# Second block's experts: PSUM banks emptied one to three chunks later in the issue order, six tiles of split halves and eight chunk buffers

## The chip, the core and the metric

The kernel runs on one core of one Trainium2 chip. The metric is the device time of the whole kernel in microseconds (us), the median of several runs. TensorE (PE) multiplies, with its weight loads shown apart (PEld); VectorE (DVE) and ScalarE (ACT) split weights and empty PSUM banks; SyncE (SP) issues the loads from HBM, in order.

## The reference, cut to what matters

Two transformer blocks in sequence on x of shape (1, 256, 1024), float32. The second block has two layers; the second of these ends in a mixture of experts, the stage at issue:

```python
D_MODEL, N_EXPERTS_2, D_FF_EXPERT, TOP_K = 1024, 8, 3584, 2

def swiglu(x, w_gate, w_up, w_down):
    return (jax.nn.silu(x @ w_gate) * (x @ w_up)) @ w_down

def moe_swiglu(x, router, w_gate, w_up, w_down):
    logits = (x @ router).astype(jnp.float32)
    top_val, top_idx = lax.top_k(logits, TOP_K)
    top_w = jax.nn.softmax(top_val, axis=-1)
    combine = jnp.sum(jax.nn.one_hot(top_idx, N_EXPERTS_2, dtype=jnp.float32) * top_w[..., None], axis=-2)
    out = jnp.zeros_like(x)
    for e in range(N_EXPERTS_2):
        out = out + combine[..., e:e + 1].astype(x.dtype) * swiglu(x, w_gate[e], w_up[e], w_down[e])
    return out
```

Each expert has 3 x 1024 x 3584 float32 weights, 44 MB, so the eight are 352 MB to be read from HBM.

## The kernel before

The kernel runs its stages one after the other; the experts of the second block are `moe2`. The router's result is ranked, and the experts are taken in the order of their token counts. The six with most tokens are **wide** (up to 128 tokens each, index p = 0 to 5), the last two are **narrow**: they share one tile of 128 rows, 64 for each.

Weights come in **chunks** of 128 x 2048 float32 (1 MB), loaded by SP into a ring of buffers `raw` (`load`, L309). For a wide expert `weights` (L346) takes a chunk and `split` (L332) makes of each half a high part `wh` (a cast on ScalarE, L340) and a low part `wl` (a subtraction on VectorE, L341), in a ring of tiles `hl`. `mm3` (L367 to L371) multiplies three times: low by high, high by low, high by high. One chunk is 12 matmuls of 512 columns. With four pairs in `hl` two chunks can be split at a time; the phase gives ten chunk buffers (six of its own, four shared), and two spare tiles (`once`) are used once each at the start.

The outer loop runs over n = 0 to 41, seven slices f of the hidden width for each of six wide experts. `up(n)` (L2007) takes four chunks: two for the gate into one bank, emptied by a Silu (L2022) into `he`; two for the up projection into a second bank, emptied by a product (L2023). `turn_h(n-1)` transposes the slice before, in the middle of `up(n)`; ScalarE and VectorE empty that bank into `hth` and `htl` (L465). `down(n-1)` (L2034) takes two chunks and adds into two banks that live for all seven slices; at the last slice `finish` splits them into `oeh`, `oel`, and `scatter` puts the rows back into x.

After 21 of the 42 steps (`thirds`, every second one, three times two in a row) stands one **narrow part** (`narrow`, L1972): gate, up or down of one slice for both narrow experts. It takes four chunks and multiplies them as float32 straight from `raw`, without a split, in 32 matmuls (L1967). A gate part is emptied by a Silu into `hn` (L1982), an up part by a product (L1984); `turn_hn` transposes `hn` and ScalarE empties that bank into `htn` (L1998).

After each chunk of `up` one piece of side work is taken from a list (`fill`): a `gather` of an expert's tokens (emptied into `xe`, L466 and L467), a transpose of a one-hot tile, or a `scatter`.

Each engine runs its own instructions strictly in the order in which they were issued, VectorE, ScalarE and SP too. That order follows from the program and from a planner's own estimate of when each instruction is ready; `behind` (L359) fixes that one instruction comes after another on its engine, without a wait. In the kernel before, nothing fixes where the emptying of a bank stands among the splits of later chunks.

Of the kernel before, what the change touches and what calls it, by code (L numbers as in the profile page):

```python
# [216 lines left out]
class _Prog:  # L217
    def __init__(self, ctx, tc, io, dump):
        self.tc, self.nc, self.io, self.dump_to = tc, tc.nc, io, dump
        nc = tc.nc  # L220
        pool = lambda name, bufs, **k: ctx.enter_context(tc.tile_pool(name=name, bufs=bufs, **k))
        self.cp = pool("cp", 1)
        self.base = pool("raw", 4)
        self.raws = [self.base] * 4
        self.hls = self.hl = [pool("hl", 4)] * 4
        self.turn_of = self.turn_hl = 0
        self.ahead, self.once = [], []
        self.rs_ins = None
# [12 lines left out]
        self.x = self.cp.tile([128, 2, D], F32, name="xres")  # L241
        self.ss = self.cp.tile([128, 2, 4], F32, name="ss_x")
        self.ss_n, self.gates = 0, []
        self.side = []
        self.first_norm = False
# [86 lines left out]
    def split(self, src):  # L332

        nc = self.nc
        pool = self.hl[self.turn_hl % len(self.hl)]
        self.turn_hl += 1
        n = src.shape[1]
        wh = pool.tile([128, 1024], F32R, name="wh")[:, :n]
        wl = pool.tile([128, 1024], F32R, name="wl")[:, :n]
        hi = nc.scalar.copy(wh, src)  # L340
        lo = nc.vector.tensor_tensor(wl, src, wh.bitcast(F32), op=ALU.subtract)  # L341
        if self.gates:
            self.behind((hi, lo), self.gates.pop(0))
        return wh, wl

    def weights(self, ap, kt):  # L346

        cols = ap.shape[2]
        w = self.load(ap.rearrange("p k c -> p (k c)"), kt * cols)
        n = kt // 2 * cols  # L350
        tiles = [self.split(w[:, i * n:(i + 1) * n]) for i in range(2)]

        def at(k, c0=0, c1=cols):
            o = k % (kt // 2) * cols
            return [t[:, o + c0:o + c1] for t in tiles[k // (kt // 2)]]

        return at

    def behind(self, ins, last):  # L359

# [1481 lines left out]
    def moe2(self):  # L1842
# [77 lines left out]
        def gather(g, k):  # L1920
            p, n, w = groups[g]
            oh = st["oh", g].rearrange("p t e s -> p t (e s)")
            ps = self.bank(self.psG if g == "f" else self.psC, "ps_ga")[:, :n * w]
            for i, (t, h) in enumerate((t, h) for t in range(2) for h in range(2)):
                ins = nc.tensor.matmul(ps, parts[h][:, t, k * 128:(k + 1) * 128], oh[:, t], start=i == 0, stop=i == 3)
                if g != "f":
                    self.behind((ins,), (self.mm_ins,))
            if g == "p":
                return nc.scalar.activation(st["xe", 6][:, k], ps, AF.Identity, scale=gain[:, k:k + 1])
            for i in range(n):  # L1930
                xe = st["xe", p + i]
                ins = self.split_evac(xe[0][:, k], xe[1][:, k], ps[:, i * 128:(i + 1) * 128], gain[:, k:k + 1])
            return ins

        def turn(p):
            ps = self.bank(self.psC, "ps_oh")
# [35 lines left out]
        def narrow(f, part):  # L1972

            both = range(2)
            if part < 2:
                ps = self.bank(self.psD, "ps_gn")
                for c in both:
                    products([ps], lambda k, sl: st["xe", 6][:, 4 * c + k, sl], 4,
                             [of("w_gu2", 6 + b, f, part, c) for b in both], c == 0, c == 1)
                if part == 0:  # L1980
                    st["hn"] = self.sp.tile([128, 512], F32, name="hn", bufs=1)
                    nc.scalar.activation(st["hn"], ps, AF.Silu)  # L1982
                    return
                nc.vector.tensor_tensor(st["hn"], st["hn"], ps, op=ALU.mult)  # L1984
                self.side.insert(0, turn_hn)
                return
            if f == 0:
                st["yd", 6] = [self.bank(self.psL, "ps_yn") for _ in both]
            for c in both:
                products(st["yd", 6], lambda k, sl: st["htn"][:, 2 * c + k, sl], 2,  # L1990
                         [of("w_d2", 6 + b, f, c) for b in both], f + c == 0, f == 6 and c == 1)
            if f == 6:
                finish(6, st["yd", 6], st["oht", 6][1])

        def turn_hn():
            ps = turned(st["hn"])
            st["htn"] = self.sp.tile([128, 4, 128], F32, name="htn", tag="hn", bufs=1)
            nc.scalar.copy(st["htn"].rearrange("p k s -> p (k s)"), ps)  # L1998

        def turned(h):  # L2000
            ps = self.bank(self.psC, "ps_ht")
# [5 lines left out]
        def up(n):  # L2007
            p, f = divmod(n, 7)
            xe = st["xe", p]
            gu = []  # L2010
            for a in range(2):
                ps = self.bank(self.psD, "ps_gu")
                for c in range(2):
                    w = self.weights(of("w_gu2", p, f, a, c), 4)
                    for k in range(4):
                        self.mm3(ps, [x[:, 4 * c + k] for x in xe], w(k), c + k == 0, c == 1 and k == 3)
                    if 2 * a + c == 1:
                        turn_h(n - 1)
                    self.fill()
                gu.append(ps)  # L2020
            h = self.sp.tile([128, 512], F32, name="he", bufs=1)
            nc.scalar.activation(h, gu[0], AF.Silu)  # L2022
            nc.vector.tensor_tensor(h, h, gu[1], op=ALU.mult)  # L2023
            st["h", n] = h

        def turn_h(n):
# [1 line left out]
                return  # L2028
            ps = turned(st["h", n])
            ht = [self.sp.tile([128, 4, 128], F32R, name="ht" + i) for i in "hl"]  # L2030
            self.split_evac(*(t.rearrange("p k s -> p (k s)") for t in ht), ps)
            st["ht", n] = ht

        def down(n):  # L2034
# [4 lines left out]
            for c in range(2):  # L2039
                w = self.weights(of("w_d2", p, f, c), 2)  # L2040
                for k in range(2):
                    for i in range(2):
                        self.mm3(yd[i], [x[:, 2 * c + k] for x in ht], w(k, i * 512, (i + 1) * 512),
                                 f + c + k == 0, f == 6 and c + k == 2)
            if f == 6:
                finish(p, yd)

        def finish(p, yd, scale=None):
            st["o", p] = []
            for c in range(2):  # L2050
                o = [self.sp.tile([128, 512], F32R, name="oe" + i, tag="oe", bufs=3) for i in "hl"]
                self.split_evac(o[0], o[1], yd[c], scale)
                st["o", p].append(o)
            self.side += [partial(scatter, p, c, t) for c in range(2) for t in range(2)]

        def scatter(p, c, t):
# [7 lines left out]
            if p == 6:  # L2064
                add = nc.vector.tensor_tensor(xo, xo, ps, op=ALU.add)
            else:
                w = comb[:, t, 0:1] if p == 0 else st["comb_o"][:, t, p:p + 1]
                add = nc.vector.scalar_tensor_tensor(xo, ps, w, xo, op0=ALU.mult, op1=ALU.add)
            if p == 5:
                st["last"] = self.squares(c, 2, (t,)), add  # L2070
# [7 lines left out]
        for n in range(43):  # L2078
# [4 lines left out]
            if n < 42:  # L2083
# [9 lines left out]
                    self.side += [partial(gather, g, k) for k in range(8)]  # L2093
                up(n)
            else:
                turn_h(n - 1)
            if n > 0:
                down(n - 1)
            if n in thirds:
                narrow(*thirds[n])  # L2100
        self.fill(99)
        self.gates = [(), st["last"], st["last"]]
# [9 lines left out]
def tile_two_blocks(ctx, tc, io, out, dump=None, start=None):  # L2112
# [15 lines left out]
    def layer1():  # L2128
        with p.phase("mix2_1", 0, **MIX2):
            p.mixer2(1)  # L2130
        with p.phase("moe2", 0, raw=6, t8=4):
            p.moe2()
        with p.phase("ple1", 2, t8=3):
            p.ple(1)
# [26 lines left out]
```

## Time and profile before

| | |
|---|---|
| median of 3 runs | 2150.38 us (2149.21 to 2150.47) |
| the profiled execution's own time | 2147.18 us |
| its span, first to last instruction | 2145.1 us |
| mean granted TensorE clock | 0.985 of full speed |
| read from HBM | 590 MB |
| the stage at issue | about 1165 to 2082 us of the span |

All times in the profile count from the first instruction. A row of a view names the line, the engine, the operation and the tiles (out<-in); a `q` behind an engine is its sequencer, which issues loads. A matmul's end is modelled: matmuls overlap, and one is drawn longer than the distance to the next.

### The profile page before, as it was taken

How to read it: one execution, taken by the hardware profiler on the slowest of the kernel's cores; microseconds unless marked ns; L12 is line 12 of the kernel's file. 1: busy time of each engine (PE TensorE's matmuls, PEld its weight loads, DVE VectorE, ACT ScalarE, POOL GpSimd, SP SyncE). 2: the span in 40 equal slices, each digit the busy share in tenths (PEclk: the TensorE clock that was granted, in tenths of full speed). 3: DMA queues.
4: the chain of work that ended last, by engine and by line, in shares of the span. 5: the costliest groups of instructions: out<-in, count | busy, mean ns of one | idle time of the engine just before them, and what ended most of it. 6: DMA issues, size and time to landing. Idle time of an engine off the chain costs nothing. (4 is left out here: it accounts for less than half of the span.)

```text
span 2145.1 us, 30558 instructions
## 1 busy us (share of the span) xinstructions
PE 2048.8 (96%) x11752; PEld 1559.7 (73%) x11752; DVE 1338.8 (62%) x1841; ACT 1142.8 (53%) x1762; POOL 113.9 (5%) x126
## 2 busy tenths in 40 slices
PE   8999899998999999989989999999999999999997
PEld 7999634337788999978878777676776667767666
DVE  5656411116787555556977777676777678767675
ACT  6555411116666444456646666565565566656664
POOL 0300000004300000004200000000000000000000
PEclk9999999999999999999998999999999999999999
DMA  7436599975314555524446899999999999989961
GB/s 292 158 118 271 188 416 425 424 315 189 140 65 177 200 194 177 183 98 166 154 159 232 321 360 379 404 385 359 369 388 367 394 389 380 377 364 390 363 267 60
DMA packets 88713, 593.14 MB, mean 277 GB/s; under 512 B 10704, under 2 KB 12528, under 8 KB 20592
## 3 DMA queue, kind: packets, MB, share of 16 engines
q1 hardware_dynamic: 88560, 591.10, 70.3%
q8 instruction: 96, 1.57, 0.3%
q14 instruction: 57, 0.47, 0.1%
HBM read 590.01 MB, written 1.05 MB: 276 GB/s over the span
## 5 line engine op out<-in xcount | busy, mean ns | idle before, releaser
L341 DVE TENSOR_TENSOR wl<-raw,wh 128x1024 fp32r<-128x1024 f32 (+1 forms) x736 | 886.0, 1229 | 297.6 <-ACT wh L340 291.9
L340 ACT CAST wh<-raw 128x1024 fp32r<-128x1024 f32 (+1 forms) x736 | 758.9, 1048 | 341.5 <-PE ps_gu L371 131.7
L369 PE MATMUL ps_gu<-wl,xe 128*128 128x512 f32 x672 | 274.8, 409 | 25.9 <-DVE wl L341 25.6
L370 PE MATMUL ps_gu<-wh,xe 128*128 128x512 f32 x672 | 266.8, 397 | 0.0
L371 PE MATMUL ps_gu<-wh,xe 128*128 128x512 f32 x672 | 266.3, 396 | 0.0
L369 PEld LDWEIGHTS ps_gu<-wl,xe 128*128 128x128 f32 x672 | 127.3, 189 | 76.9 <-DVE wl L341 41.9
L371 PEld LDWEIGHTS ps_gu<-wh,xe 128*128 128x128 f32 x672 | 127.3, 189 | 29.6
L370 PEld LDWEIGHTS ps_gu<-wh,xe 128*128 128x128 f32 x672 | 127.6, 190 | 25.1
L369 PE MATMUL ps_yd<-wl,hth 128*128 128x512 f32 x336 | 133.2, 398 | 1.2 <-ACT hth L465 1.2
L370 PE MATMUL ps_yd<-wh,htl 128*128 128x512 f32 x336 | 132.7, 395 | 0.6 <-DVE htl L465 0.6
L371 PE MATMUL ps_yd<-wh,hth 128*128 128x512 f32 x336 | 132.6, 395 | 0.0
L369 PE MATMUL ps_fg<-xtl,wh 128*128 128x256 f32 x448 | 126.3, 282 | 0.7 <-DVE ffs L1825 0.4
L371 PE MATMUL ps_fg<-xth,wh 128*128 128x256 f32 x448 | 125.8, 281 | 0.0
L370 PE MATMUL ps_fg<-xth,wl 128*128 128x256 f32 x448 | 125.8, 281 | 0.0
L1062 PE MATMUL ps_gu<-raw,xe 128*64 128x512 f32 x376 | 101.3, 596 | 0.0
L1967 PE MATMUL ps_gn<-raw,xp 128*64 128x512 f32 x448 | 100.3, 596 | 0.0
L398 POOL TENSOR_TENSOR rs<-rs_v,neghalf 128x2 f32<-128x2 f32 x11 | 8.4, 760 | 1712.7 <-DVE rs_v L396 1405.9
L369 PEld LDWEIGHTS ps_fg<-xtl,wh 128*128 128x128 f32 x448 | 84.3, 188 | 2.4 <-DVE ffs L1825 0.6
L371 PEld LDWEIGHTS ps_fg<-xth,wh 128*128 128x128 f32 x448 | 84.3, 188 | 1.1
L370 PEld LDWEIGHTS ps_fg<-xth,wl 128*128 128x128 f32 x448 | 84.2, 188 | 1.2
L1967 PEld LDWEIGHTS ps_gn<-raw,xp 128*64 128x64 f32 x448 | 31.2, 137 | 61.1 <-issue 58.8
L369 PEld LDWEIGHTS ps_yd<-wl,hth 128*128 128x128 f32 x336 | 63.0, 188 | 16.3 <-ACT hth L465 1.4
(636 smaller groups left out, 4005.9 us busy)
## 6 DMA issues: line engine op xcount, KB each, us to landing
raw<-in_w_gu SPq DMA_DIRECT2D x269, 1024.0 KB, 8.0
raw<-in_w_d SPq DMA_DIRECT2D x135, 1024.0 KB, 8.6
raw<-in_w_in SPq DMA_DIRECT2D x39, 1024.0 KB, 4.9
raw<-in_w_fg SPq DMA_DIRECT2D x14, 1024.0 KB, 4.9
raw<-in_w_fu SPq DMA_DIRECT2D x14, 1024.0 KB, 4.7
raw<-in_w_fd SPq DMA_DIRECT2D x14, 1024.0 KB, 4.8
raw<-in_w_out SPq DMA_DIRECT2D x12, 1024.0 KB, 4.9
wh<-in_w_gu SPq DMA_DIRECT2D x16, 512.0 KB, 12.0
```

The lines of the kernel that those rows point to most:

```text
L340: hi = nc.scalar.copy(wh, src)
L341: lo = nc.vector.tensor_tensor(wl, src, wh.bitcast(F32), op=ALU.subtract)
L369: nc.tensor.matmul(out, lhs[0], rhs[1], start=first, stop=False)
L370: nc.tensor.matmul(out, lhs[1], rhs[0], start=False, stop=False)
L371: self.mm_ins = nc.tensor.matmul(out, lhs[0], rhs[0], start=False, stop=last)
L398: self.rs_ins = nc.gpsimd.tensor_tensor(dst, v[:, :n], self.neghalf[:, :n], op=ALU.pow)
L1062: nc.tensor.matmul(ps[64 * b:64 * b + 64], xs(k, b), ws[b][k // 2][:, k % 2 * 512:(k % 2 + 1) * 512], start=first and k == 0, stop=last an ...
L1967: ins = nc.tensor.matmul(out[i][sl], xs(k, sl), ws[b][:, (n * k + i) * 512:(n * k + i + 1) * 512], start=first and k == 0, stop=last and k ...
```

## The change

What empties a bank is no longer issued where the bank's matmuls are. It goes into a list (`later`) with a number of chunks; `weights` counts that number down after the splits of each later chunk, and issues what is due behind these splits on its engine (`run_late`, `behind`). `ahead`, half the split tiles in `hl`, is three. Products and Silus of `up` and what empties `turn_h` and `turn_hn` get a number of 2, a narrow part's Silu and product 3, gathers and scatters 1, the two halves of `finish` 1 and 2. The last expert's scatter is emptied at once as before. `moe2` gets two more pairs of split tiles (six, three chunks) and two chunk buffers less of its own (four, eight in all; the same memory). `turn_hn` moves from the first free filler to the place behind the fourth chunk of the next `up`; one filler moves from `up` to `down`. The bank of `ps_gu` is taken after the first chunk's splits. Before the first narrow part, all side work is done and all that is late is issued.

```diff
@@ split, weights @@
+        self.last_split = hi, lo
...
         tiles = [self.split(w[:, i * n:(i + 1) * n]) for i in range(2)]
+        self.run_late()
...
+    def later(self, chunks, do):
+        self.late.append([chunks, do])
+
+    def run_late(self, whole=False):
+        due, self.late = self.late, []
+        for n, do in due:
+            if whole or n <= 1:
+                for ins in do():
+                    self.behind((ins,), (self.last_split[0 if ins.ins.engine == mybir.EngineType.Activation else 1],))
+            else:
+                self.late.append([n - 1, do])
@@ gather @@
+            if g == "f":
+                return empty()
+            self.later(1, empty)
@@ narrow, turn_hn @@
-                    nc.scalar.activation(st["hn"], ps, AF.Silu)
+                    self.later(ahead, lambda: (nc.scalar.activation(st["hn"], ps, AF.Silu),))
...
-                nc.vector.tensor_tensor(st["hn"], st["hn"], ps, op=ALU.mult)
-                self.side.insert(0, turn_hn)
+                self.later(ahead, lambda: (nc.vector.tensor_tensor(hn, hn, ps, op=ALU.mult),))
+                turns.append(turn_hn)
...
-            nc.scalar.copy(st["htn"].rearrange("p k s -> p (k s)"), ps)
+            self.later(ahead - 1, lambda: (nc.scalar.copy(htn.rearrange("p k s -> p (k s)"), ps),))
@@ up @@
                     w = self.weights(of("w_gu2", p, f, a, c), 4)
+                    if c == 0:
+                        ps = self.bank(self.psD, "ps_gu")
...
                         turn_h(n - 1)
-                    self.fill()
-                gu.append(ps)
-            nc.scalar.activation(h, gu[0], AF.Silu)
-            nc.vector.tensor_tensor(h, h, gu[1], op=ALU.mult)
+                    elif 2 * a + c == 3 and turns:
+                        turns.pop(0)()
+                    else:
+                        self.fill()
+                if a == 0:
+                    self.later(ahead - 1, lambda ps=ps: (nc.scalar.activation(h, ps, AF.Silu),))
+                else:
+                    self.later(ahead - 1, lambda ps=ps: (nc.vector.tensor_tensor(h, h, ps, op=ALU.mult),))
@@ turn_h, down, finish @@
-            self.split_evac(*(t.rearrange("p k s -> p (k s)") for t in ht), ps)
+            self.later(ahead - 1, lambda: self.split_evac(*(t.rearrange("p k s -> p (k s)") for t in ht), ps))
...
+                if c == 0:
+                    self.fill()
...
-                self.split_evac(o[0], o[1], yd[c], scale)
+                self.later(1 + c, lambda o=o, y=yd[c]: self.split_evac(o[0], o[1], y, scale))
@@ scatter @@
+            if p == 5:
+                st["last"] = *empty(), self.squares(c, 2, (t,))
+            else:
+                self.later(1, empty)
+        turns, ahead = [], len(self.hl) // 2
@@ the loop over n @@
+                self.run_late(True)
                 turn_h(n - 1)
+                self.run_late(True)
...
             if n in thirds:
+                if thirds[n] == (0, 0):
+                    self.fill(99)
+                    self.run_late(True)
                 narrow(*thirds[n])
+        self.run_late(True)
         self.fill(99)
@@ layer1 @@
-        with p.phase("moe2", 0, raw=6, t8=4):
+        with p.phase("moe2", 2, raw=4, t8=4):
```

## Rows read from the trace of the kernel before

**Rows 1.** The page: TensorE over the span; its granted clock in 40 slices.

```profile
PE 2048.8 (96%) x11752; PEld 1559.7 (73%) x11752; DVE 1338.8 (62%) x1841; ACT 1142.8 (53%) x1762; POOL 113.9 (5%) x126
...
PEclk9999999999999999999998999999999999999999
```

**Rows 2.** Busy time of each engine in three stretches; clock, DMA share, GB/s last.

```profile
350.00:400.00 50.00, 49.76 (x232) 20.27 (x230) 6.29 (x11) 8.07 (x18) 0.00 (x0) 1.00 1.02 423
...
1200.00:2000.00 800.00, 779.85 (x3489) 555.12 (x3489) 574.94 (x570) 494.43 (x566) 0.00 (x0) 1.00 0.94 378
...
1165.00:2082.00 917.00, 891.05 (x3988) 639.65 (x3987) 668.90 (x668) 571.12 (x655) 0.00 (x0) 1.00 0.93 371
```

**Rows 3.** TensorE's waits, 1165 to 2082 us: us in total, times, longest.

```profile
PE ps_gu L369 <- DVE wl L341: 25.6, 21, 2.1
```

**Rows 4.** Waits of all engines, 1165 to 2082 us.

```profile
DVE hn L1984 <- PE ps_gn L1967: 61.0, 7, 10.0
...
ACT hn L1982 <- PE ps_gn L1967: 56.6, 7, 10.2
ACT htn L1998 <- PE ps_ht L2003: 47.2, 5, 13.0
...
ACT hth L465 <- PE ps_ht L2003: 21.0, 13, 2.2
```

**Rows 5.** Timeline round 1502 us, VectorE then TensorE: start, length, [idle before].

```profile
1502.01 0.69 DVE L1984 TENSOR_TENSOR hn<-hn,ps_gn 128x512 f32<-128x512 f32 x1 [8.81 <-PE ps_gn L1967]
1502.61 3.49 DVE L341 TENSOR_TENSOR wl<-raw,wh 128x1024 fp32r<-128x1024 f32 x3
...
1499.62 2.31 PE L1967 MATMUL ps_gn<-raw,xp 128*64 128x512 f32 x10
1503.89 0.51 PE L369 MATMUL ps_gu<-wl,xe 128*128 128x512 f32 x1 [1.95 <-DVE wl L341]
```

**Rows 6.** Timeline round 1593 us, ScalarE then TensorE.

```profile
1592.88 0.60 ACT L1982 ACTIVATE hn<-ps_gn 128x512 f32<-128x512 f32 x1 [10.21 <-PE ps_gn L1967]
1593.38 3.88 ACT L340 CAST wh<-raw 128x1024 fp32r<-128x1024 f32 x4
...
1585.72 7.09 PE L1967 MATMUL ps_gn<-raw,xp 128*64 128x512 f32 x32
1592.74 0.50 PE L369 MATMUL ps_gu<-wl,xe 128*128 128x512 f32 x1
1593.08 0.39 PE L370 MATMUL ps_gu<-wh,xe 128*128 128x512 f32 x1
...
1594.00 0.40 PE L371 MATMUL ps_gu<-wh,xe 128*128 128x512 f32 x1
1595.73 0.50 PE L369 MATMUL ps_gu<-wl,xe 128*128 128x512 f32 x1 [1.33 <-DVE wl L341]
```

**Rows 7.** Timeline round 1690 us, ScalarE then TensorE.

```profile
1688.75 0.59 ACT L465 CAST hth<-ps_ht 128x512 fp32r<-128x512 f32 x1 [2.17 <-PE ps_ht L2003]
...
1692.09 0.50 PE L369 MATMUL ps_gu<-wl,xe 128*128 128x512 f32 x1 [0.57 <-DVE wl L341]
```

**Rows 8.** Groups by form, 1165 to 2082 us: count | busy us, mean ns | idle before.

```profile
L341 DVE TENSOR_TENSOR wl<-raw,wh 128x1024 fp32r<-128x1024 f32 x486 | 577.8, 1221 | 145.1 <-ACT wh L340 140.1
L340 ACT CAST wh<-raw 128x1024 fp32r<-128x1024 f32 x486 | 502.7, 1051 | 177.0 <-PE ps_gu L371 130.1 <-PE ps_yd L371 42.9 <-DVE wl L341 1.4
...
L465 DVE TENSOR_TENSOR htl<-ps_ht,hth 128x512 fp32r<-128x512 f32 x41 | 28.1, 686 | 10.7 <-ACT hth L465 10.7
...
L465 ACT CAST hth<-ps_ht 128x512 fp32r<-128x512 f32 x41 | 23.8, 582 | 21.0 <-PE ps_ht L2003 21.0
...
L466 ACT ACTIVATE xe<-ps_ga,gcols 128x128 fp32r<-128x128 f32 x40 | 13.8, 361 | 17.0 <-PE ps_ga L1925 14.5 <-DVE xe L467 2.5
```

**Rows 9.** SP's waits, 1200 to 2080 us; landing of `raw`, 1200 to 2000 us.

```profile
SPq L309 <- PE ps_gn L1967: 103.1, 30, 6.9
...
DMA to landing us min/median/max: 4.7/7.8/13.1
```

More of the change, by code (lines that the diff above doesn't have):

```diff
@@ L244, in __init__ @@
         self.side = []
+        self.late, self.last_split = [], None
         self.first_norm = False
@@ L1927, in gather, with empty @@
                     self.behind((ins,), (self.mm_ins,))
[L1928 to L1933, printed above, removed]
+            def empty():
+                if g == "p":
+                    return nc.scalar.activation(st["xe", 6][:, k], ps, AF.Identity, scale=gain[:, k:k + 1]),
+                ins = ()
+                for i in range(n):
+                    xe = st["xe", p + i]
+                    ins += self.split_evac(xe[0][:, k], xe[1][:, k], ps[:, i * 128:(i + 1) * 128], gain[:, k:k + 1])
+                return ins
+            if g == "f":
+                return empty()
+            self.later(1, empty)
         def turn(p):
@@ L1981, in narrow @@
                     st["hn"] = self.sp.tile([128, 512], F32, name="hn", bufs=1)
-                    nc.scalar.activation(st["hn"], ps, AF.Silu)
+                    self.later(ahead, lambda: (nc.scalar.activation(st["hn"], ps, AF.Silu),))
                     return
-                nc.vector.tensor_tensor(st["hn"], st["hn"], ps, op=ALU.mult)
-                self.side.insert(0, turn_hn)
+                hn = st["hn"]
+                self.later(ahead, lambda: (nc.vector.tensor_tensor(hn, hn, ps, op=ALU.mult),))
+                turns.append(turn_hn)
                 return
@@ L1996, in turn_hn @@
             ps = turned(st["hn"])
-            st["htn"] = self.sp.tile([128, 4, 128], F32, name="htn", tag="hn", bufs=1)
-            nc.scalar.copy(st["htn"].rearrange("p k s -> p (k s)"), ps)
+            htn = st["htn"] = self.sp.tile([128, 4, 128], F32, name="htn", tag="hn", bufs=1)
+            self.later(ahead - 1, lambda: (nc.scalar.copy(htn.rearrange("p k s -> p (k s)"), ps),))
         def turned(h):
@@ L2009, in up @@
             xe = st["xe", p]
-            gu = []
+            h = self.sp.tile([128, 512], F32, name="he", bufs=1)
             for a in range(2):
-                ps = self.bank(self.psD, "ps_gu")
                 for c in range(2):
                     w = self.weights(of("w_gu2", p, f, a, c), 4)
+                    if c == 0:
+                        ps = self.bank(self.psD, "ps_gu")
                     for k in range(4):
@@ L2018, in up @@
                         turn_h(n - 1)
-                    self.fill()
-                gu.append(ps)
-            h = self.sp.tile([128, 512], F32, name="he", bufs=1)
-            nc.scalar.activation(h, gu[0], AF.Silu)
-            nc.vector.tensor_tensor(h, h, gu[1], op=ALU.mult)
+                    elif 2 * a + c == 3 and turns:
[6 more added lines that the diff above has]
+                    self.later(ahead - 1, lambda ps=ps: (nc.vector.tensor_tensor(h, h, ps, op=ALU.mult),))
             st["h", n] = h
@@ L2063, in scatter, with empty @@
             xo = self.x[:, t, c * 512:(c + 1) * 512]
-            if p == 6:
-                add = nc.vector.tensor_tensor(xo, xo, ps, op=ALU.add)
-            else:
[L2067 to L2070, printed above, removed]
+            def empty():
+                if p == 6:
+                    return nc.vector.tensor_tensor(xo, xo, ps, op=ALU.add),
+                w = comb[:, t, 0:1] if p == 0 else st["comb_o"][:, t, p:p + 1]
+                return nc.vector.scalar_tensor_tensor(xo, ps, w, xo, op0=ALU.mult, op1=ALU.add),
+            if p == 5:
+                st["last"] = *empty(), self.squares(c, 2, (t,))
+            else:
+                self.later(1, empty)
+        turns, ahead = [], len(self.hl) // 2
         thirds = {round(2 + 1.85 * i): divmod(i, 3) for i in range(21)}
@@ L2099, in moe2 @@
             if n in thirds:
+                if thirds[n] == (0, 0):
+                    self.fill(99)
+                    self.run_late(True)
                 narrow(*thirds[n])
+        self.run_late(True)
         self.fill(99)
-        self.gates = [(), st["last"], st["last"]]
+        add, sq = st["last"]
+        self.gates = [(), (sq, add), (sq, add)]
         flat = lambda a: a.rearrange("p k c -> p (k c)")
```

## Prediction

> **What bounds the kernel now.** The page comes first, to see that no engine's total settles the matter: TensorE is drawn busy for 96% of the span, and its granted clock is full, 2.4 GHz, in nearly every slice [rows 1]. A drawn matmul is longer than the distance to the next, so that share hides short waits. The windows say where the change acts: the second block's experts run from about 1165 to 2082 us, 917 us long, with TensorE drawn busy for 891, VectorE for 669 and ScalarE for 571 [rows 2]. VectorE and ScalarE have a quarter and more to spare; the transfers carry 378 GB/s from 1200 to 2000 us, where another stage of the same kernel carries 423 [rows 2]. So TensorE sets the end of this stage, and what can be won is what it stands still. The list of waits gives that directly: 21 waits, 25.6 us, all before a matmul that reads a low part of the weights, all ended by the subtraction that makes it [rows 3].
>
> The same list, for the other engines, says why a subtraction that needs only a landed chunk and a free tile is late. VectorE stood 61.0 us before the seven products `hn`, ScalarE 56.6 us before the seven Silus of `hn`, 47.2 us before `htn` and 21.0 us before `hth`, each time until TensorE had filled the bank [rows 4]. These engines take their queue in order, so everything behind such an instruction waits too. The timeline shows it three times. At 1502.01 VectorE begins a product it had waited 8.81 us for, and only then three subtractions; TensorE, done with the narrow part at 1501.93 (1499.62 plus 2.31), starts at 1503.89, 1.95 us later [rows 5]. At 1592.88 it is a Silu on ScalarE, 10.21 us waited, four casts behind it, and TensorE runs dry after half a chunk for 1.33 us [rows 6]. At 1688.75 it is `hth`, 2.17 us waited, and TensorE loses 0.57 us [rows 7].
>
> **How much that is in TensorE's own time.** Matmuls of a chunk follow each other at 0.23 us (from 1593.08 to 1594.00 it is four steps, 0.92) but are drawn 0.39 to 0.40 us long [rows 6]. A wait inside a stream therefore costs more than is drawn: 1594.00 to 1595.73 is 1.73, less 0.23 is 1.50 for 1.33 drawn. After a narrow part it costs 0.07 more than drawn, as the unwaited start at 1592.74 lies 0.07 before the drawn end of the part before it (its 32 matmuls are drawn 7.09 long). Between 0.07 and 0.17 for each of 21 is 1.5 to 3.6; I take 2.4. The removable time is 25.6 + 2.4 = 28.0 us, and without it the stage's TensorE work is 917 - 28 = 889 us.
>
> **The change, part by part.** *Issue order.* The Silu and product of `gu`, those of `gn`, `hth`/`htl`, `htn`, the gathers', `finish`'s and `scatter`'s are no longer issued where their matmuls are, but behind the splits of one, two or three later chunks. No instruction is added or taken away: 42 Silus, 42 products and so on remain. What counts is whether an instruction now waits for something its followers don't. With three chunks of split tiles, the splits of chunk c+3 need chunk c finished. A bank filled by chunk c and emptied behind the splits of c+2 (the value for `gu` and `hth`) thus waits for nothing that the next splits don't wait for too. Narrow parts stand after chunk c and are emptied behind the splits of c+3; the next splits, of c+4, need c+1, which comes after the part. So all three kinds of wait above should go. What is late next: after `hth` (0.58 us) and `htl` (0.69) [rows 8], issued when chunk 1 of an `up` ends, `down` needs them two chunks, 12 x 0.23 = 2.8 us each, later: 5.6 us for 0.2 + 0.58 + 0.69. The splits behind it (cast 1.05, subtraction 1.22 [rows 8]) follow with some 2 us to spare. Cost 0; if the cover were gone it would be 1.5 us for each of 42, 62 us.
>
> *The short lags.* Gathers, scatters and the first half of `finish` get a lag of one chunk only. Such an instruction waits for work after chunk c while it holds up the splits of c+2, which otherwise could start before. Count from the end of the gather: 0.2 us for the signal, two casts of `xe` at 0.36, one cast of weights at 1.05, one subtraction at 1.22, is 3.2 us; TensorE comes to c+2 after 2.8. That is 0.4 to 0.5 us for each of the 16 gathers of two experts, 8 us, and some 0.3 for each of six `finish`, 2 us. From below the bound is 0: of TensorE's waits now not one is charged to an `xe` [rows 3]. The instruction may also be placed later than the rule asks, as now. I take 2 us, nearer the row, and keep 0 to 10.
>
> *Six split tiles.* Beside what they do above, splits may run one chunk further ahead, which absorbs VectorE's extras; that is already in the 28.0. A gain beyond it is excluded, as 889 us is matmul work at its pitch.
>
> *Eight chunk buffers instead of ten.* The loads are issued on SP's queue in order, each when its buffer is free. Chunks in flight are 8 + 3 instead of 10 + 2, and a narrow part holds four of the eight until TensorE has used them; the queue already stands 103.1 us at that [rows 9]. When a narrow part starts, the next four chunks are in (three split, one raw), the fifth is issued when the part's first half is done, at 3.5 us, and lands 4.7 us later at the earliest [rows 9], at 8.2. It is wanted at 7.0 + 4 x 2.8 less 2.5 for its split, at 15.7. So 7 us to spare; the prefetch at the stage's start falls from 12 chunks (two spare tiles counted) to 10, still 28 us of TensorE's work. In throughput: 378 x 800 us is 302 MB; without the 24 us of the waits that lie in that stretch (28 less 4) it is 302 MB in 776 us, 390 GB/s, against 423 shown [rows 2]. Cost 0 to 4 us of jitter; I take 1.
>
> *Moved side work.* One filler goes from each `up` to `down`, `turn_hn` from the first chunk to the fourth, and before the first narrow part all fillers are flushed (two transposes). Same count on TensorE: 0.
>
> **Sum.** 28.0 - 2 - 1 = 25.0 us. The profiled execution took 2147.2 us around a span of 2145.1, 3.2 below the median of the runs (2150.4). Own time 2147.2 - 25.0 = 2122; median 2150.4 - 25.0 = **2125 us**.
>
> **A rule against it.** The stretch from 350 to 400 us moved 423 GB/s with full queues [rows 2]; the stage at issue needs 390. The Trainium skill, HBM Reference, Specifications, gives a core a share of about 358 GB/s, and about 425 when it streams alone. By the share, 302 MB would take an estimated 845 us, longer than the 800 measured here, so the trace contradicts it for this run; the figure for a lone core agrees with 423. By the share nothing could be won.
>
> **Rivals.**
> - *Half of it.* The lags of one chunk block as worked out (10 us) and the loads' jitter takes 4: 28 - 14 = 14, 2136 us. For it: in-order queues did exactly this [rows 4]. Against: no wait of TensorE is charged to `xe` now.
> - *The transfers are the bound.* The DMA engines are busy 94% of 1200 to 2000 us at 378 GB/s [rows 2]. If a shorter gap only made TensorE wait for landings, the time stays: 2150 us. Against: at the same rate per busy share, 378 / 0.94 = 402 GB/s would still do for 390, and TensorE has no wait for a landing in [rows 3]. (This is what the share of the HBM Reference, above, would make of it.)
> - *Slower: SP's queue behind the narrow part.* With four of eight buffers held, SP can't issue the fifth chunk for up to 3.5 us into each of 21 parts; if the fourth had landed early, the DMA engines idle up to 7 us per part. 302 MB at 423 takes 715 us, so 61 us of idling are free, 3 us for each of the 20 parts in that stretch; from 4.3 us (61 plus today's 24, over 20) it is slower than before, and at 7 it is 715 + 140 = 855, 55 more than now: 2205 us. Against: a queue that is behind has no such gap, and 7 us of lead stand between.
> - *Slower: a bank comes free too late.* A narrow part's bank is next wanted by the third chunk after it, 5.6 us on, and is emptied some 0.9 us after the part if the splits of that third chunk are through. If these are late by over 5 + 2 us at each of the 14 parts that fill a bank, more than 28 us is lost: 2155 us or more. The Trainium skill, PSUM — Partial Sum Buffer, Summary, asks to evacuate promptly; the trace of before shows the opposite harm, an evacuation issued too soon.
>
> **Chances.** Forecast (2117 to 2133) 0.60; half 0.20; transfers 0.09; queue 0.08; bank 0.03. Predicted 2125 us. The range reaches down to the whole 28 and some clock regained after fewer stops (2116), and up over the half case to 2146, which leaves out no more than 0.2. About 0.2%, 4.3 us, is what a measurement of this kernel can tell from no change. Faster by more: 0.60 + 0.20 = 0.80; within: 0.09; slower: 0.11.
>
> **What would show it.** In the profile after: the 25.6 us of waits of TensorE for the subtraction shrink to a few us; the waits of VectorE and ScalarE before `hn` remain about as long, but with all splits of three chunks done before them, and TensorE goes from a narrow part to the next chunk without a gap; `hth` comes behind the splits of the fourth chunk. DMA share in the stage rises to 96% or more. Wrong, if TensorE waits for `xe` or `oeh` casts' followers, for a landing of `raw`, or for a bank after a narrow part; or if the loads' time to landing falls to 4.7 us with SP waiting on the narrow parts, which is the queue rival.

## The result and the profile after

The changed kernel takes 2121.6 us (median of four runs, 2118.5 to 2123.3) against 2149.8 us (four runs, 2149.05 to 2150.5): the ratio is 0.987, 95% interval 0.985 to 0.988, 28.2 us less. 2125 us, faster, was forecast. The profiled execution took 2123.05 us around a span of 2121.3. One execution of a later version (the third subtraction held back, below) took 3379.8 us at a granted clock of 0.556 and is left out of that version's median. Lines have moved: `mm3` is L387 to L389, cast and subtraction are L341 and L342, `hth`/`htl` L483, the narrow matmuls L1991, the Silu and product of `hn` L2006 and L2009.

The list of TensorE's waits of the changed kernel, from 1165 to 2055 us (us in total, times, longest), answers to [rows 3]:

```profile
PE ps_ga L1943 <- DVE oh L1924: 4.3, 1, 4.3
PE ps_yd L387 <- ACT hth L483: 0.8, 1, 0.8
PE ps_ga L1943 <- DVE htl L483: 0.6, 1, 0.6
```

All 21 waits for a subtraction of weights are gone. A new one stands there, 4.3 us long, before a gather; it comes back below. In the windows of the same kernel (columns as in [rows 2]) TensorE is drawn busy for 798.6 of the 800 us from 1200 to 2000, where it was 779.9, and the transfers carry 388 GB/s:

```profile
1165.00:2059.00 894.00, 888.25 (x3994) 643.27 (x3993) 665.48 (x677) 559.94 (x657) 0.00 (x0) 1.00 0.93 381
1200.00:2000.00 800.00, 798.59 (x3602) 574.10 (x3602) 592.37 (x590) 498.10 (x586) 0.00 (x0) 1.00 0.94 388
```

The stage's length is read below from its first weight matmul to the last scatter's: before, 1149.14 to 2099.93 us, 950.8 us; after, 1152.25 to 2076.07 us, 923.8 us, 27.0 us less. Nothing else of the kernel was changed, and the place where the stage starts differs from profile to profile, so this length compares better than the total.

**The same places as before.** The timeline of the changed kernel round the narrow part of [rows 5], VectorE and then TensorE:

```profile
1497.31 6.90 DVE L342 TENSOR_TENSOR wl<-raw,wh 128x1024 fp32r<-128x1024 f32 x6
1505.77 0.69 DVE L2009 TENSOR_TENSOR hn<-hn,ps_gn 128x512 f32<-128x512 f32 x1 [1.56 <-PE ps_gn L1991]
...
1498.61 7.09 PE L1991 MATMUL ps_gn<-raw,xp 128*64 128x512 f32 x32
1505.62 0.51 PE L387 MATMUL ps_gu<-wl,xe 128*128 128x512 f32 x1
```

Six subtractions, three chunks, are done during the narrow part, and only then does VectorE wait for its bank. TensorE goes on at 1505.62, 0.08 us before the drawn end of the part (1498.61 plus 7.09): the start without a wait that the prediction read in [rows 6]. The narrow part of [rows 6] itself, ScalarE and then TensorE:

```profile
1594.36 0.60 ACT L2006 ACTIVATE hn<-ps_gn 128x512 f32<-128x512 f32 x1 [5.29 <-PE ps_gn L1991]
1595.92 1.05 ACT L341 CAST wh<-raw 128x1024 fp32r<-128x1024 f32 x1 [0.97 <-PE ps_gu L389]
...
1594.22 0.51 PE L387 MATMUL ps_gu<-wl,xe 128*128 128x512 f32 x1
1596.88 0.40 PE L389 MATMUL ps_gu<-wh,xe 128*128 128x512 f32 x1
1597.11 0.40 PE L387 MATMUL ps_gu<-wl,xe 128*128 128x512 f32 x1
```

ScalarE still waits 5.29 us for the bank, but the cast behind it waits for TensorE to free a tile, not the other way round: from 1596.88 to 1597.11 TensorE goes into the next chunk at its step of 0.23 us.

The waits of ScalarE and VectorE in the changed kernel, from 1165 to 2055 us, beside [rows 4]:

```profile
ACT hth L483 <- PE ps_ht L2028: 57.0, 31, 2.6
ACT wh L341 <- DMA raw<-in_w_gu: 56.9, 29, 6.5
ACT hn L2006 <- PE ps_gn L1991: 24.5, 6, 6.1
ACT htn L2023 <- PE ps_ht L2028: 6.9, 6, 1.2
...
DVE hn L2009 <- PE ps_gn L1991: 11.1, 5, 4.4
```

The waits before `hn` and `htn` are shorter, those before `hth` longer; of them only `hth` reaches TensorE, once, for 0.8 us. The cast now waits 29 times for a chunk's landing, up to 6.5 us. That too stays ahead of TensorE, but it is the margin that went: over the wide experts' chunks whose first matmul lies between 1200 and 2000 us, the shortest time from landing to first matmul was 14.7 us before and is 6.9 us after. For the chunks of narrow parts, which need no split, it was 11.9 us and is 5.8 us.

**The new stop.** The timeline of the changed kernel at the second step: VectorE, then TensorE.

```profile
1179.15 0.28 DVE L1896 TENSOR_REDUCE rk_o<-hot_t 128x16 f32<-128x128 f32 x1
1179.35 2.35 DVE L342 TENSOR_TENSOR wl<-raw,wh 128x1024 fp32r<-128x1024 f32 x2
1181.97 0.42 DVE L1924 TENSOR_TENSOR oh<-consts,rk_o 128x256 fp32r<-128x256 f32 x1
...
1177.71 0.40 PE L389 MATMUL ps_gu<-wh,xe 128*128 128x512 f32 x1
1182.44 0.47 PE L1943 MATMUL ps_ga<-oh,xsh 128*128 128x128 f32 x1 [4.33 <-DVE oh L1924]
```

At the stage's start VectorE also ranks the experts, a chain of small operations that ends in the one-hots of the narrow pair (L1924). With six split tiles free, pairs of subtractions stand between the links of that chain, and the one-hots come 29.7 us after the stage's first matmul. In the kernel before single subtractions stood there, and the one-hots came after 18.4 us:

```profile
1165.76 0.28 DVE L1878 TENSOR_REDUCE rk_o<-hot_t 128x16 f32<-128x128 f32 x1
...
1166.04 1.22 DVE L341 TENSOR_TENSOR wl<-raw,wh 128x1024 fp32r<-128x1024 f32 x1
...
1167.52 0.41 DVE L1906 TENSOR_TENSOR oh<-consts,rk_o 128x256 fp32r<-128x256 f32 x1
```

In the changed kernel TensorE stands from 1177.71 to 1182.44, 4.73 us less a step of 0.23. Behind the stop the granted clock is lower, 1.2 GHz in a part of the two windows (last three columns of the changed kernel's windows: clock, DMA share, GB/s); before, both had the full clock.

```profile
1175.00:1185.00 10.00, 5.67 (x26) 4.71 (x24) 7.96 (x19) 4.05 (x6) 0.00 (x0) 0.87 0.41 152
1185.00:1200.00 15.00, 15.00 (x63) 12.27 (x63) 9.15 (x9) 9.16 (x14) 0.00 (x0) 0.86 0.68 253
```

0.13 of 10 us and 0.14 of 15 are 3.4 us of work. With the stop it is some 8 us lost at this place. Over the whole stage, though, the lower clock cost about as much as before, 4.9 us of work against 4.8: the kernel before was at half clock in the stage's first 6.1 us and for 3.4 us at 2005, the changed kernel in its first 2.9 us and for 6.8 us behind the stop.

### The profile page after: what moved, and what is told of

It is laid out like the page before. It is cut to its first block, busy times and chain, and to the rows that moved or that the text cites. A ratio compares the mean times of both kernels' runs of the same rounds, so it can differ in the third digit from the quotient of the medians.

```text
span 2121.3 us, 30529 instructions
## 1 busy us (share of the span) xinstructions
PE 2046.0 (96%) x11752; PEld 1564.1 (74%) x11752; DVE 1334.4 (63%) x1841; ACT 1130.3 (53%) x1762; POOL 113.9 (5%) x126
## 5 line engine op out<-in xcount | busy, mean ns | idle before, releaser
L342 DVE TENSOR_TENSOR wl<-raw,wh 128x1024 fp32r<-128x1024 f32 (+1 forms) x736 | 879.3, 1229 | 287.0 <-ACT wh L341 284.1
L341 ACT CAST wh<-raw 128x1024 fp32r<-128x1024 f32 (+1 forms) x736 | 743.8, 1047 | 335.8 <-PE ps_gu L389 85.5
L387 PE MATMUL ps_gu<-wl,xe 128*128 128x512 f32 x672 | 272.1, 405 | 0.0
L389 PE MATMUL ps_gu<-wh,xe 128*128 128x512 f32 x672 | 265.9, 396 | 0.0
L387 PEld LDWEIGHTS ps_gu<-wl,xe 128*128 128x128 f32 x672 | 127.3, 189 | 42.8 <-issue 12.2
L389 PEld LDWEIGHTS ps_gu<-wh,xe 128*128 128x128 f32 x672 | 127.0, 189 | 29.6
L387 PE MATMUL ps_yd<-wl,hth 128*128 128x512 f32 x336 | 133.1, 400 | 1.4 <-ACT hth L483 1.4
L389 PE MATMUL ps_yd<-wh,hth 128*128 128x512 f32 x336 | 132.5, 394 | 0.0
L387 PE MATMUL ps_fg<-xtl,wh 128*128 128x256 f32 x448 | 126.3, 282 | 0.7 <-DVE ffs L1843 0.4
L389 PE MATMUL ps_fg<-xth,wh 128*128 128x256 f32 x448 | 125.8, 281 | 0.0
L1991 PE MATMUL ps_gn<-raw,xp 128*64 128x512 f32 x448 | 99.4, 595 | 0.0
L387 PEld LDWEIGHTS ps_fg<-xtl,wh 128*128 128x128 f32 x448 | 84.3, 188 | 2.4 <-DVE ffs L1843 0.6
L389 PEld LDWEIGHTS ps_fg<-xth,wh 128*128 128x128 f32 x448 | 84.3, 188 | 1.1
L1991 PEld LDWEIGHTS ps_gn<-raw,xp 128*64 128x64 f32 x448 | 30.9, 137 | 60.6 <-issue 60.6
L387 PEld LDWEIGHTS ps_yd<-wl,hth 128*128 128x128 f32 x336 | 62.9, 188 | 16.0 <-ACT hth L483 1.9
## 6 DMA issues: line engine op xcount, KB each, us to landing
wh<-in_w_gu SPq DMA_DIRECT2D x16, 512.0 KB, 11.9
```

The costliest lines, as they stand in the source:

```text
L387: nc.tensor.matmul(out, lhs[0], rhs[1], start=first, stop=False)
L389: self.mm_ins = nc.tensor.matmul(out, lhs[0], rhs[0], start=False, stop=last)
L1991: ins = nc.tensor.matmul(out[i][sl], xs(k, sl), ws[b][:, (n * k + i) * 512:(n * k + i + 1) * 512], start=first and k == 0, stop=last and k ...
```

## The experiments

The theory that went in: TensorE's waits came from the order of issue; with it right, the six tiles matter only because a lag of one chunk would hold up the splits at each of the 42 steps. The rival: the tiles let the splits run ahead, and do it alone. Three numbers describe most versions: chunks of split tiles, chunk buffers, and the lags in chunks of the narrow parts' `hn` and of `he`, `htn`, `hth`/`htl` (0 is at once, as before). Before is 2, 10, 0 and 0; the changed kernel is 3, 8, 3 and 2. The side work that the change moved, and the later place where the bank of `ps_gu` is taken, are in every version but the first and have no run of their own. Runs of one group share a chip and the runs of the kernel before.

**First group: the two halves of the change, and two lags.** (Before: 2149.84 us, seven runs.)

Tiles and buffers alone, in the kernel before (3, 8, 0, 0):

```diff
-        with p.phase("moe2", 0, raw=6, t8=4):
+        with p.phase("moe2", 2, raw=4, t8=4):
```

> The kernel before with nothing but six split tiles and eight chunk buffers; the issue order is left to the planner. If the gain comes from the order in which banks are emptied, most of TensorE's 28 us of standing still stays, because a Silu or product of a narrow part still stands in front of splits: 2138 to 2152 us, TensorE waits for the low parts of 15 us or more. If the third chunk of split tiles alone absorbs these waits: 2118 to 2126 us.

Measured: 2160.3 us (2158.5 to 2164.7), ratio 1.006 (1.004 to 1.008), 10.5 us slower. TensorE's waits in this run, 1165 to 2050 us:

```profile
PE ps_gu L369 <- DVE wl L341: 22.8, 20, 2.0
PE ps_ga L1925 <- DVE oh L1906: 4.4, 1, 4.4
```

The old waits are nearly all there: a free tile is no use to a subtraction that stands behind a product waiting for its bank. And the stop before the gather has come with the tiles. The stage is 963.5 us long, 12.7 more; the stop is 4.5 of it, and 7.1 went to the lower clock, which cost the stage 11.8 us of work here and 4.8 before. Both expectations lie below the result: neither had a loss in it.

The order alone, with the tiles and buffers of before (2, 10, 2, 1):

```diff
-        with p.phase("moe2", 2, raw=4, t8=4):
+        with p.phase("moe2", 0, raw=6, t8=4):
```

> The changed kernel with the four split tiles and ten chunk buffers of before; the lags shrink with the tiles, to two chunks for a narrow part and one for the rest. If the order alone is what pays: 2120 to 2127 us. My theory says that lag and tiles belong together: a narrow part's waits go (some 20 us), but what empties the transposed slice then stands behind one chunk's splits and in front of the next, which TensorE wants 2.8 us later; that cost 0.75 us at seven places before (0.57 drawn) and would now come in each of 42 steps, 31 us, so 2145 to 2160 us, with TensorE waiting for the low parts at about 40 places.

Measured: 2125.9 us (2123.3 to 2133.9), ratio 0.990 (0.987 to 0.993), 24 of the 28 us. The theory fell here: it wanted a stop at each of 42 steps. The waits of this run, TensorE's and ScalarE's before `hth`, and one stop with the `hth` ahead of it:

```profile
PE ps_gu L387 <- DVE wl L342: 7.5, 13, 0.6
...
ACT hth L483 <- PE ps_ht L2028: 27.2, 13, 2.6
...
1617.15 0.59 ACT L483 CAST hth<-ps_ht 128x512 fp32r<-128x512 f32 x1 [2.18 <-PE ps_ht L2028]
...
1620.49 0.50 PE L387 MATMUL ps_gu<-wl,xe 128*128 128x512 f32 x1 [0.59 <-DVE wl L342]
```

Thirteen stops. Eleven of them come some 3.3 us behind the start of an `hth` for which ScalarE had waited 2.2 us, as the one shown. The first two lie at the stage's start, at 1165 and 1169 us, before any `hth`; the kernel before has two there as well. Two more waits for `hth` stopped nothing, and in the other 29 steps ScalarE came to `hth` after the transposes were done. There is no stop before the gather.

The changed kernel with all but `hn` emptied at once (3, 8, 3, 0). Shown is the helper and one of seven places, which all got a lag of 0 (gathers, scatters, `finish`, `htn`, `he` twice, `hth`):

```diff
     def later(self, chunks, do):
+        if not chunks:
+            do()
+            return
...
-            self.later(ahead - 1, lambda: self.split_evac(*(t.rearrange("p k s -> p (k s)") for t in ht), ps))
+            self.later(0, lambda: self.split_evac(*(t.rearrange("p k s -> p (k s)") for t in ht), ps))
```

> The changed kernel with only the narrow parts' Silu and product issued late (three chunks); all else that empties a bank is issued at once, as before, and placed by the planner. The waits after narrow parts are 7 of about 2.0 us and 5 of 1.5 us of the kernel before, 21 us of 28; if they are the bulk: 2122 to 2131 us, with some waits of 0.6 us behind hth left. If every lag is needed: 2140 us or more.

Measured: 2137.45 us (2133.2 to 2138.8), ratio 0.995 (0.993 to 0.997), between the two. Its waits (lines are three further down):

```profile
PE ps_gu L390 <- DVE wl L342: 6.4, 9, 2.1
PE ps_ga L1946 <- DVE oh L1927: 4.3, 1, 4.3
PE ps_gu L390 <- ACT he L2053: 2.3, 2, 1.2
...
ACT htn L2026 <- PE ps_ht L2031: 6.0, 6, 1.2
```

The long waits behind the narrow gate and up parts are gone with `hn` late alone; nine remain, the longest behind the last narrow part, whose bank `finish` empties. The two before `he` are for a bank that came free late. ScalarE's wait before `htn`, emptied at once here, is 6.0 us where [rows 4] had 47.2: the late `hn` and the moved `turn_hn` go together in this run, and none tells them apart.

All lags one chunk (3, 8, 1, 1):

```diff
-                    self.later(ahead, lambda: (nc.scalar.activation(st["hn"], ps, AF.Silu),))
+                    self.later(1, lambda: (nc.scalar.activation(st["hn"], ps, AF.Silu),))
...
-            self.later(ahead - 1, lambda: self.split_evac(*(t.rearrange("p k s -> p (k s)") for t in ht), ps))
+            self.later(1, lambda: self.split_evac(*(t.rearrange("p k s -> p (k s)") for t in ht), ps))
```

> The changed kernel with every lag set to one chunk, tiles and buffers as changed. If any fixed place behind later splits is enough: 2119 to 2127 us. If the lag has to match the number of chunks that can be split, what empties the transposed slice holds up the next splits by 0.6 + 0.2 + 0.58 + 0.60 us, casts and subtraction follow (1.05 + 1.22), 4.3 us against 3.4 that TensorE needs to get there: 0.75 to 0.9 us in each of 42 steps, 31 to 38 us: 2150 to 2162 us.

Measured: 2133.6 us (2130.5 to 2136.8), ratio 0.993 (0.991 to 0.995).

```profile
PE ps_gu L387 <- DVE wl L342: 6.0, 11, 0.6
PE ps_ga L1943 <- DVE oh L1924: 4.3, 1, 4.3
```

Eleven stops, not 42, and a time between the two expectations. Each stop follows an `hth` for which ScalarE had waited; ten are 0.56 to 0.59 us long, one 0.2. A lag of one is enough for `hn`. So `hn` needs a lag, `hth` needs two chunks, and the third chunk of tiles has done nothing yet but bring the stop before the gather.

**Second group: the new theory, the new stop, the margin.** (Before: 2148.55 us, nine runs.) The changed kernel beside them:

> The changed kernel once more, beside the others on the same chip, so that differences of a few us from it can be read: 2118 to 2124.

Measured: 2125.1 us (2121.35 to 2125.9), 1 us above the range expected; its stage is 922.5 us long.

Two chunks of tiles, ten buffers, lags of two (2, 10, 2, 2), made from the changed kernel; one of the four places where `ahead - 1` became 2 is shown:

```diff
-            self.later(ahead - 1, lambda: self.split_evac(*(t.rearrange("p k s -> p (k s)") for t in ht), ps))
+            self.later(2, lambda: self.split_evac(*(t.rearrange("p k s -> p (k s)") for t in ht), ps))
...
-        with p.phase("moe2", 2, raw=4, t8=4):
+        with p.phase("moe2", 0, raw=6, t8=4):
```

> Two chunks of split tiles and ten buffers as before the change, the new order of issue, and he, hth/htl and htn with a lag of two chunks in place of one. In the run with the order alone (lag one) TensorE stopped 13 times, each 0.98 us from matmul to matmul where 0.23 is its step: 13 x 0.75 = 9.8 us, and ScalarE waited for the transposes before 13 of 42 hth. Theory (a bank may be emptied behind the splits that wait for the same chunk anyway, and the added tiles are needed only because the lags were tied to their number): the 13 stops go, and there is no stop before the narrow gather: 2125.9 - 9.8 = 2116, range 2112 to 2120. Rival (with two chunks of split tiles some evacuation must stand ahead of a split that TensorE wants next, so that the third pair of tiles is what removes the stops): stops of 0.5 to 1 us remain at 10 or more places, 2122 to 2130.

Measured: 2116.3 us (2111.1 to 2120.6), ratio 0.986 (0.9845 to 0.9875), 9 us under the changed kernel beside it. When it ran again in the third group it took 2114.25 us (2111.2 to 2117.9), ratio 0.983 (0.982 to 0.984). TensorE's waits from 1155 to 2070 us:

```profile
PE ps_yd L387 <- ACT hth L483: 1.2, 1, 1.2
PE ps_yd L388 <- DVE htl L483: 0.6, 1, 0.6
PE ps_sc L2091 <- DVE xres L2099: 0.6, 2, 0.5
PE ps_gu L387 <- DVE wl L342: 0.6, 1, 0.6
PE ps_sc L2091 <- DVE oel L483: 0.2, 1, 0.2
```

The window of this run that answers to [rows 2]:

```profile
1200.00:2000.00 800.00, 800.00 (x3600) 575.20 (x3599) 606.35 (x591) 514.97 (x586) 0.00 (x0) 1.00 0.96 391
```

TensorE is drawn busy without a break for 800 us. Twelve of the 13 stops are gone, all behind `hth` among them; the one that is left lies at the stage's start. The stop before the gather is not there; the stage is 917.1 us long in both runs, 6.8 less than in the changed kernel's profile (5.5 less than in its second one). Adding tiles was not needed for the gain.

The narrow pair's one-hots put ahead of the next subtraction, in the changed kernel:

```diff
-                places("p")
+                self.gates = [((), places("p"))]
```

> In the changed kernel TensorE stands 4.3 us at 1177.7 us before the gather of the paired narrow experts, because their one-hots are made only at 1181.97 us, behind subtractions that run ahead; behind it the granted clock is at half for 6.83 us, 3.4 us of work. Theory (this stop and the clock behind it are a loss that the two added split tiles brought): with the first subtraction behind the one-hots both go, and the time is 7 to 8 us less than the changed kernel's, 2113 to 2118. Rival (VectorE's work before that point is what is late, and it only changes places): TensorE stands as long for a subtraction instead, and the time stays at 2119 to 2124.

Measured: 2123.95 us (2122.05 to 2124.3): nothing won. TensorE's wait in this run:

```profile
1170.55 0.76 PE L387 MATMUL ps_gu<-wl,xe 128*128 128x512 f32 x1 [4.34 <-DVE wl L342]
```

The stop has moved to the subtraction that was held back and kept its length. The rival was right about this order.

The changed kernel with six chunk buffers:

```diff
-        with p.phase("moe2", 2, raw=4, t8=4):
+        with p.phase("moe2", 2, raw=2, t8=4):
```

> The changed kernel with two chunk buffers fewer, six in place of eight. In the traces the shortest time from a chunk's landing to its first matmul is 14.7 us before and 6.9 us after the change. Two buffers are two chunks less in flight, 2 x 2.8 = 5.6 us. Theory of the prediction (the eight buffers leave a margin of about 7 us, most of which the two would use up): few or short stops, 2121 to 2130. Rival that transfers are nearly the bound already with eight: TensorE waits for splits that wait for landings at most narrow parts, 1 to 3 us at 20 places, 2140 to 2180. Rival that SP's queue behind the narrow parts decides: 2180 or more.

Measured: 2128.6 us (2127.2 to 2131.7), 3.5 over the changed kernel beside it. ScalarE's and TensorE's waits, 1165 to 2050 us:

```profile
ACT wh L341 <- DMA raw<-in_w_gu: 201.6, 82, 11.4
...
PE ps_gu L387 <- DVE hn L2009: 3.4, 3, 1.6
PE ps_yd L387 <- DVE wl L342: 0.8, 1, 0.8
PE ps_gu L387 <- DVE wl L342: 0.5, 1, 0.5
```

The shortest time from landing to first matmul (wide experts) is 2.4 us here and 6.9 with eight, 4.4 less for two buffers. Most of the new waits are not for weights but for a bank: the product of `hn` stands behind splits that have become late, and the bank comes free too late, 3.4 us in three places. Two stops for weights hold 1.3 us.

**Third group.** (Before: 2151.57 us, nine runs.) The third subtraction held back instead of the first:

```diff
-                places("p")
+                self.gates = [((), ()), ((), ()), ((), places("p"))]
```

> As the run with the one-hots first, but the third subtraction of the second step stands behind them instead of the first, so that the chunk that TensorE comes to next is split in time. In that run the stop of 4.3 us only moved, from the gather (1177.7) to the subtraction that was held back (TensorE left without work from 1166.2 us, the subtraction at 1169.19 behind the one-hots at 1168.86). Theory (the stop is a matter of order alone): no stop at either place, 4.3 us and the 3.4 us of clock behind it won, 2114 to 2119. Rival (at the stage's start VectorE has too much to do for both, whatever the order): a stop of 2 to 4 us for one or the other, 2120 to 2126.

Measured: 2120.2 us (median of four, 2117.1 to 2122.9), ratio 0.985 (0.983 to 0.986). In its stage the wait is shorter and still there, and one for a subtraction has come:

```profile
PE ps_ga L1943 <- DVE oh L1924: 1.8, 1, 1.8
...
PE ps_gu L387 <- DVE wl L342: 0.5, 1, 0.5
```

The stage is 920.9 us long, 1.7 to 3 less than with the change. So part of the stop is order; this experiment doesn't settle whether the rest is.

The run with two chunks of tiles and lags of two, now with eight buffers (2, 8, 2, 2; the edit against that run), and with ten again:

```diff
-        with p.phase("moe2", 0, raw=6, t8=4):
+        with p.phase("moe2", 0, raw=4, t8=4):
```

> The run with two chunks of split tiles and lags of two chunks, with eight chunk buffers in place of ten: two chunks less in flight than in that run, one less than in the changed kernel. Theory (the time from landing to first matmul there, about 14 us in the chunks looked at, can give 5.6 us): as with ten, 2112 to 2120. Rival (its gain over the changed kernel comes from the two buffers, not from the order): 2121 to 2128, with waits for splits that wait for landings.

> The run with two chunks of split tiles and lags of two chunks once more, beside the other two on the same chip: 2111 to 2121.

Measured: 2117.7 us (2113.3 to 2121.7), ratio 0.984 (0.982 to 0.985), and 2114.25 us as told above. Stages of 918.4 and 917.1 us: the two buffers are worth 1.3 us there; the rest of the 3.4 us between the medians lies within their spread. The shortest time from landing to first matmul is 6.8 us with eight and 11.6 to 11.7 with ten.

## Why the prediction was right, point by point

**The bound and the 28.0 us.** Right. All 21 waits are gone; counted from matmul to matmul, less the step, they held 28.6 us. The order of issue did it, with the side work that moved along: without the tiles it gave 24 us, and with lags of two in place of one 32 us or more. The Trainium skill, PSUM — Partial Sum Buffer, Engine vs sequencer instructions, says that the queues of ScalarE and VectorE are strictly first in, first out; the trace agrees: in [rows 5] three subtractions ran only after a product that VectorE had waited 8.81 us for, and now six run ahead of that product.

**Short lags, 2 us.** Mis-sized; it measured nothing. No wait of TensorE behind a gather's `xe` or a scatter is in the list after. The working gave 8 us as the most that the gathers could cost; the row (no `xe` in TensorE's waits) was the better guide. The same count made my first theory expect 42 stops in the run with the order alone; eleven of that kind came, because ScalarE often reached `hth` after the transposes were done.

**Six split tiles: "a gain beyond is excluded".** What failed here is what was left out beside the gain: a loss, put at nothing without a reason. The tiles let subtractions stand between the small operations that make the one-hots, at 4.5 us of stop and 3.4 us at the lower clock behind it (1.7 us in the second profile of the same kernel). In one form or another the stop is in every run with six tiles, and in none of the four with four (order alone; two chunks of tiles with ten buffers, twice, and with eight). What the tiles do give is small: two waits at the stage's start, 1.1 us of the 25.6, are gone with six tiles and stay, both or one, in the runs with four. The Trainium skill, Perfetto Trace Analysis, Optimization Strategy, says that a gap that repeats on the engine that should be saturated can mean too little room for the next tile; the run with the tiles alone speaks against it here, 10.5 us slower with 20 waits still there.

**Eight buffers: 1 us, 7 us to spare.** The cost was about right (two buffers are worth 1.3 us of stage in the runs with four tiles), the margin too large. The prediction's 7.5 us are counted after 2.5 us for the split, which makes 10 us from landing to first matmul; the least measured is 6.9. Two buffers fewer cost 3.5 us. SP's waits before the buffers of the narrow gate and up parts (changed kernel, 1165 to 2055 us) are 125.0 us where [rows 9] had 103.1:

```profile
SPq L310 <- PE ps_gn L1991: 125.0, 28, 10.8
```

The landing of `raw` in the changed kernel, 1200 to 2000 us:

```profile
DMA to landing us min/median/max: 4.7/9.3/15.7
```

The queue rival would have shown landings falling to 4.7 us; the median rose from 7.8 to 9.3. The transfers rival is out: 388 GB/s here and 391 in the run with two chunks of tiles, against the 390 worked out. The DMA share of 96% or more was wrong for the changed kernel, 0.94 with more bytes per busy time, and right for that run. The share of about 358 GB/s that the Trainium skill, HBM Reference, Specifications, gives a core is passed in both.

**A bank that comes free too late.** Not behind a narrow part of the changed kernel. The one wait of the kind there is 0.6 us before a gather: it is released by `htl`, which the gather doesn't read, so it is for the bank. In the run with six buffers it is the largest of the new waits, where the splits are late by a landing. The mechanism was right, its condition was not met.

**`hth` and `htl` later, cost 0.** Right: 31 waits of ScalarE before `hth`, 57.0 us, and one wait of TensorE for it, 0.8 us. **"About as long" for the waits before `hn`** was wrong, 61.0 to 11.1 us and 56.6 to 24.5 us: the engines come to them later, with three chunks split.

**The sum.** 28.0 - 2 - 1 = 25.0 was forecast; the medians gave 28.2 and the stage 27.0. By the terms: the 21 waits held 28.6, the lags cost nothing, and the buffers show no wait of their own. Not foreseen were the new stops, 4.5 us before the gather and 0.8 before another. The lower clock, 4.9 us of work in the stage after and 4.8 before, takes nothing from the difference. So 23.3 would have been due, and some 3.7 us more were won. The distances between matmuls of the chunks that lie from 0.245 to 0.5 us, too short to be listed as waits, account for 3 of it (12.6 us over the step before, 9.7 after, those at half clock counted in both); why they fell, and the rest, stays open. That the sum came so near is thus partly luck: a loss of 5 us that was left out stands against 3.7 us that nobody had counted and 2 us for lags that cost nothing.

## What to carry to other kernels

Where an engine both feeds TensorE and empties its banks in one queue, issue the emptying behind the feed that waits for the same point anyway; read from the trace which instruction the late feed stood behind, not only which engine released the wait. More tiles don't help a feed that stands behind such an instruction, and they let it run ahead of small work that something else needs soon: try the order first, by itself. When a lag or a buffer count is tied to another size in the code, test them apart.

## What the runs showed of the hardware

One stop of 4.3 us cost 8 at its place: behind it the granted clock was 0.87 and 0.86 in the windows of 10 and 15 us. In all eight profiles with six tiles TensorE stops here, for 1.8 to 4.4 us, and the clock falls to 1.2 GHz in the stop or right behind it, at 3.4 us of work in five and 1.7 in three; in the five profiles with four tiles it does not fall there. The run with the tiles alone had 20.5 us at half clock behind the stage's first 3.1, in five places: behind that stop, and behind four of its seven stops of about 2 us. The kernel before had 3.4 us behind its stage's first 6.1, behind one of seven such stops.

The place where the stage starts, behind stages that no version changed, went from 1146.5 to 1155.6 us over the profiles. It goes roughly along with the time at the lower clock ahead of it. Up to 1160 us that clock cost 17.1 us of work where the stage began at 1146.5 (two chunks of tiles, ten buffers), 25.6 at 1149.1 (before), 29.0 at 1152.25 (the changed kernel) and 33.4 at 1155.6 (two chunks of tiles, eight buffers), but 18.8 at 1150.7 (all lags one) and 22.2 at 1152.4 (six buffers). The four profiles with ten buffers start at 1146.5 to 1149.1, the eight with eight at 1146.8 to 1155.6; whether the buffers, which change what is loaded ahead of the stage, have a part in it, no run tells. So two medians a few us apart say less than the length of the stage.
